# Gate rows written from SyncE's queue, eight weight tiles asked for from ScalarE's

## The chip, the core and the metric

The kernel runs on one core of a Trainium2 chip (trn2). Its time is the device time in microseconds (us) of one execution, as the median of several runs. The engines are named as the profile names them: PE is TensorE's matmul, PEld its weight load, DVE VectorE, ACT ScalarE, POOL GpSimd, SP SyncE. DMA transfers are asked for on three queues, which the profile numbers: q1 is SP's, q10 is ACT's, q0 is POOL's. An engine that asks for a transfer spends time of its own on that (its issue); the data move later, on 16 DMA engines which all queues share.

## The reference

One layer on 256 tokens of width 2048: a retention group beside a recurrent group, cross-attention over 256 memory rows, a PEER feed-forward, and a final norm. The change lies in PEER. For each token 8 heads pick 16 of 16384 single-neuron experts by product keys:

```
sub_scores = jnp.einsum('thcd,hckd->thck', q, sub_keys)
vals, ids = lax.top_k(sub_scores, PEER_TOPK)
cand = vals[:, :, 0, :, None] + vals[:, :, 1, None, :]
top_sc, pos = lax.top_k(cand.reshape(t, PEER_HEADS, ...), PEER_TOPK)
eid = (i1 * PEER_N_KEYS + i2).reshape(t, PEER_HEADS * PEER_TOPK)
gate = jax.nn.softmax(top_sc, axis=-1).reshape(t, PEER_HEADS * PEER_TOPK)
...
act = jax.nn.gelu(jnp.einsum('td,tkd->tk', xb, u_tab[eb]))
out = jnp.einsum('tk,tkd->td', gb * act, v_tab[eb])
```

## The kernel before

The tables are U and V, 16384 rows of 2048 each, taken as 128 columns of 128 experts. The kernel computes the first `RD = 40` columns for every token whether or not they were picked ("the eager pass"), then up to 32 more columns chosen by how often they were picked, and gathers the remaining picked rows one by one.

**The eager pass of U** (`u_chunk`, `u_block`, lines 1190 and 151) takes the 40 columns as 80 weight tiles of 128 x 1024 f32, 512 KB each. A tile is loaded into one of four `raw` buffers (`raw_tile`, line 128, on SP's queue); ACT casts it to a high half (line 137), DVE makes the low half (line 138), and PE multiplies both (line 158, 24 matmuls a tile). Two tiles make a column; ACT then applies gelu (line 1198). A `raw` buffer is free again when the low half of its tile is made, so a tile is asked for up to four tiles ahead of its use.

**The weave.** After each half column (one tile) `wv.pump` runs some of the waiting side work, generators that yield what they cost: the credit is `RG = 8.0` a tile while the gates are built, and 3.5 (`RK`) in the stage behind it. First in this queue is `route` with `gbuild`, then `side`.

**`gbuild`** (line 1131) builds the gates of all tokens, 64 steps of 4 tokens. A step compares indices on DVE (line 1149), scales on POOL (1150), casts on ACT (1152), multiplies on PE (1163 gates, 1166 counts) and copies the product out on ACT (1169, 1170). It costs 1.3 and 0.3 of credit. Eight steps are a group of 32 tokens (`GT`), and at its end (step `m % 8 == 7`, line 1171) the group's gates go to DRAM in three writes: `gd` (line 1173, 384 KB) and twice `rows`, a view of `gt` (lines 1175 and 1176, 384 KB and 1024 KB, in runs of 32 floats). So there are 8 groups and 24 writes, all on ACT's queue. A group then scales two finished columns on DVE (line 1181, 0.3 of credit each).

**`side`** (line 1117) follows: `choose` picks the 32 further columns; `look_up` (line 1009) finds in 8 steps, 4 for each half of the tokens, which picks these cover. Before it, POOL loads index rows of 1 MB each (`at_load`, line 1005: steps 0 to 3 early, 4 and 5 as `side` starts, 6 and 7 behind look-ups 0 and 1, into the buffers of look-ups 0 and 1). Each look-up is 32 matmuls (line 1017) and two DVE operations (1023, 1025). The normed rows `hn` are read back in two reads of 1 MB on SP's queue, into buffers that a look-up has read before: `h[0]` behind the fourth look-up (line 1021) and one of the `kept` tiles behind the sixth (line 1027). Behind each half of the look-ups DVE picks the rows still to be gathered (lines 941 and 942), and POOL gathers the first three of them, 1 MB each (line 1063, issued at line 1474). The 33rd column (tiles 65 and 66) may get its gelu only once all look-ups are done (line 1196). The products of these rows with the normed tokens (line 1481) come later and read `h[0]`.

**Order.** In this part of the kernel no order is written out by hand: the framework's planner takes the program in the order in which it was emitted and puts an instruction into its engine's queue where, by the planner's own estimate, its inputs and buffers are ready; among ready ones the earlier emitted goes first. On the chip each engine works its queue in that order, and one that waits holds all behind it. The part from line 1813 on is ordered by hand, and is not touched.

Of the kernel before, what the change touches and what calls it, by code (L numbers as in the profile page):

```python
# [18 lines left out]
P = 128  # L19
D = 2048  # L20
KB = D // P
T = 256
# [18 lines left out]
SPILL_AT = (8, 14)  # L41
LOOK_AT = (20, 30, 40, 50)
EARLY = 3
SWAP = 8
WARM = 18
RD = 40
# [6 lines left out]
GT = 32  # L53
# [36 lines left out]
def hybrid_layer_kernel(ctx: ExitStack, tc: tile.TileContext, a: dict, out: bass.AP, dbg=None):  # L90
    nc = tc.nc
    V, A, G, PE = nc.vector, nc.scalar, nc.gpsimd, nc.tensor
# [21 lines left out]
    def slot(tag, shape, name, dt=F32):  # L114
        return b8.tile(shape, dt, tag=tag, name=name, bufs=3 if tag == "ms" else 2)
# [5 lines left out]
    def sm(name):  # L121
        return ps2_.tile([P, 512], F32, tag="sm", name=name)
# [2 lines left out]
    iota = cp.tile([P, P], F32, name="iota")  # L125
    ones = cp.tile([P, P], F32, name="ones")

    def raw_tile(src):
        t = ws.tile([P, 1024], F32, tag="raw", name="raw", bufs=4)
        nc.sync.dma_start(t, src)  # L130
        return t

    def split(raw, hi=None, lo=None):
# [17 lines left out]
    def u_block(srcs, pt):  # L151
        for j, src in enumerate(srcs):
            hi, lo = split(raw_tile(src))
            for part in range(3):
                for k in range(8):
                    kb = 8 * j + k
                    x = xn[:, kb, T:] if part == 1 else xn[:, kb, :T]
                    PE.matmul(pt[:, :T], (lo if part == 2 else hi)[:, k * P:(k + 1) * P], x,  # L158
                              start=(part == 0 and kb == 0), stop=(part == 2 and kb == KB - 1))
            wv.pump(wv.rate)  # L160

    def whalf(j, src, xt, pt, raw=None):
        hi, lo = split(raw_tile(src) if raw is None else raw)
        w_mms(j, hi, lo, xt, pt)
        wv.pump(wv.rate)
# [329 lines left out]
    for i in range(3):  # L495
        t = slot("qs" if i == 0 else "ms", [P, TT, 1024], "qkv"[i])
# [321 lines left out]
    def route():  # L818
# [76 lines left out]
        for tt in range(TT):  # L895
# [31 lines left out]
            yield from finish(tt)  # L927
        wv.rate = RG
        gates = gbuild()
        tr["t"] = rp.tile([P, P + 1], F32, tag="cand", name="tri")  # L930
        nc.sync.dma_start(tr["t"], a["tri"])
# [59 lines left out]
    def at_of(i):  # L991
        return ats[i].bitcast(BF16).rearrange("p (s t) -> p s t", t=P)

    def compare(i):
        at = at_of(i)
        for n in range(0, 32, 16):
            V.tensor_scalar(at[:, n:n + 16], at[:, n:n + 16], tr["t"][:, P:], None, op0=ALU.is_equal)
            yield 0.7
# [6 lines left out]
    def at_load(i):  # L1005
        tt, c = divmod(i, 4)
        G.dma_start(ats[i].bitcast(BF16), i1d[tt, 32 * c:32 * c + 32].rearrange("s t -> (s t)")[None, :].to_broadcast([P, 32 * P]))

    def look_up(tt):
        fl = gx["b"][:, 1920:2048]  # L1010
        for c in range(4):
            at = at_of(4 * tt + c)
            if tt:
                yield from compare(4 * tt + c)
            pt = sm("look")
            for n in range(32):
                PE.matmul(pt[:, NW * n:NW * n + NW], at[:, n], words, start=True, stop=True)
            if not tt and c < 2:
                at_load(6 + c)
            if 4 * tt + c == 3:  # L1020
                nc.sync.dma_start(h[0], hn[:P, :])
            found = gx["b"][:, 512:512 + 32 * NW].rearrange("p (s w) -> p s w", w=NW)
            V.tensor_tensor(found, pt[:, :32 * NW].rearrange("p (s w) -> p s w", w=NW),
                            which[tt][:, 32 * c:32 * c + 32], op=ALU.mult)
            V.tensor_reduce(fl[:, 32 * c:32 * c + 32], found, axis=AX.X, op=ALU.add)
            if 4 * tt + c == 5:
                nc.sync.dma_start(held_in[NCH + NDY - 1], hn[P:2 * P, :])
            yield 1.0
        fu = fl.bitcast(U32)
        V.tensor_copy(fl.bitcast(I32), fl)  # L1030
        V.tensor_tensor(fu, fu, bits[tt], op=ALU.logical_shift_right)
        V.tensor_scalar(fu, fu, 31, None, op0=ALU.logical_shift_left)
        for t in (key[tt], work[tt]):
            V.tensor_tensor(t.bitcast(U32), t.bitcast(U32), fu, op=ALU.bitwise_or)
        yield 1.0
# [90 lines left out]
    gd = dp.tile([NCH - ND, P, T // GT, 8, GT], F32, name="gd")  # L1126
# [4 lines left out]
    def gbuild():  # L1131
        prev = None
        cnt["t"] = pcn.tile([P, 512], F32, tag="cnt", name="cnt")
        rows = gt_.rearrange("(r p) t -> p r t", p=P)
        for n in range(T // 4 + 1):
            if n in LOOK_AT:
                yield from compare(LOOK_AT.index(n))
            nxt = None
            tt, t0 = divmod(4 * n, P)
            ss = slice(t0, t0 + 4)  # L1140
            if n < T // 4:
                h0, q0 = n % 3 * 512, n % 3 * 256
                four = gx["b"][:, 1536:1792].bitcast(BF16).rearrange("p (a b) -> p a b", b=4)
                o1 = gx["a"][:, h0:h0 + 512].rearrange("p (a b) -> p a b", a=4)
                c1, o2 = (gx["d"][:, k + q0:k + q0 + 256].bitcast(BF16).rearrange("p (a b) -> p a b", b=4)
                          for k in (0, 768))
                og = gx["b"][:, h0:h0 + 512].rearrange("p (a b) -> p a b", a=4)
                for o, ix in ((o2, rT), (c1, i1T)):
                    V.tensor_tensor(o, four, ix[tt][:, None, ss].to_broadcast([P, P, 4]), op=ALU.is_equal)  # L1149
                G.tensor_tensor(og, o2.rearrange("p a b -> p b a"), gtT[tt][:, ss, None].to_broadcast([P, 4, P]),  # L1150
                                op=ALU.mult)
                A.copy(o1, c1.rearrange("p a b -> p b a"))
                nxt = (o1, o2, og, c1)
                yield 1.3
            if prev:
                o1, o2, og, c1 = prev
                m = n - 1
                k = m % (GT // 4)
                if k == 0:
                    ga, gb = slot("qs", [P, P // 2, GT], "gs"), gbs[m // (GT // 4) % 2]  # L1160
                pt = sm("G")
                for j in range(4):
                    PE.matmul(pt.rearrange("p (c t) -> p c t", t=4)[:, :, j], o1[:, j], og[:, j],  # L1163
                              start=True, stop=True)
                for j in range(4):
                    PE.matmul(cnt["t"][:, :RS], c1[:, :, j], o2[:, RD:, j], start=(m == 0 and j == 0),  # L1166
                              stop=(m == T // 4 - 1 and j == 3))
                ks = slice(4 * k, 4 * k + 4)
                A.copy(ga[:, :, ks], pt[:, :T].rearrange("p (c t) -> p c t", t=4))
                A.copy(gb[:, :, ks], pt[:, T:].rearrange("p (c t) -> p c t", t=4))  # L1170
                if k == GT // 4 - 1:
                    ts = slice(4 * m + 4 - GT, 4 * m + 4)
                    A.dma_start(gd[:, :, m // (GT // 4)].rearrange("q p c t -> p q c t"),
                                ga[:, 8 * ND:RD].rearrange("p (q c) t -> p q c t", c=8))
                    A.dma_start(rows[:, :P // 2 - RD, ts], ga[:, RD:])
                    A.dma_start(rows[:, P // 2 - RD:, ts], gb)
                    for i in range(ND):
                        while f"u{i}" not in done:
                            yield 3.0
                        av = acts[i][:, :, ts]  # L1180
                        V.tensor_tensor(av, ga[:, 8 * i:8 * i + 8], av, op=ALU.mult)
                        yield 0.3
                yield 0.3
            prev = nxt
        done.add("gbuild")
# [294 lines left out]
    def dot(tt, k, gat, last, k0=0, rows=None):  # L1480
        V.scalar_tensor_tensor(junk, gat, 1.0, h[0] if rows is None else rows, op0=ALU.mult, op1=ALU.mult, accum_out=coef[tt][:, k:k + 1])  # L1481
        if k % 8 == 7 or k == last:
            s = slice(max(k - k % 8, k0), k + 1)
            A.activation(coef[tt][:, s], coef[tt][:, s], AF.Gelu_apprx_tanh)
            V.tensor_tensor(coef[tt][:, s], coef[tt][:, s], sel2[tt][:, s], op=ALU.mult)
# [20 lines left out]
    def chosen():  # L1506
# [19 lines left out]
        for kind, tt, k, gs in ops:  # L1526
# [8 lines left out]
            if kind == "dot":  # L1535
                dot(tt, k, mine[0], BASE - 1, rows=held_in[NCH + NDY - 1] if tt and k < SWAP else None)
                if tt == 0 and k == BASE - 1:
# [231 lines left out]
    row_ops = chosen()  # L1769
    for _ in range(EARLY):  # L1770
        next(row_ops)
# [138 lines left out]
```

## Time and profile before

| | |
|---|---|
| median of 3 runs | 1966.1 us (1964.4 to 1967.62) |
| the profiled execution | 1966.72 us |
| its span, first to last instruction | 1964.9 us |
| mean granted TensorE clock | 0.985 |
| the three lines of gate writes, first and last issue | 1031.7 and 1158.7 us |
| bytes moved by DMA | 502.01 MB, mean 255 GB/s |
| chain that ended last, by engine | PE 62%, DMA 16%, DVE 9%, issue 7%, POOL 3% |

All times of the trace count from the span's start. A row of a timeline gives the start, the duration, the engine (with a q where it is the engine's queue that issues a DMA), the line, the operation, what it writes and reads, and in brackets the idle time before it and what ended that. "raw<-in_U_dram" is a load of a U tile, "gd<-gs" and "gt<-gs" are the gate writes, "h<-hn" and "kept<-hn" the reads of normed rows, "kept<-i1d" and "h<-i1d" the index rows, "U<-xn,hi" the products of the eager pass. In rows by stage the first number is the stage's length, then follow the busy times of PE, PEld, DVE, ACT and POOL with the instructions in parentheses, the granted clock, the DMA engines' share and GB/s.

### The profile page before, as it was taken

To read this page: it belongs to the slowest core of one execution; us is meant where nothing else is said; L and a number is where in the kernel's file an instruction comes from. 1 tells how busy PE (TensorE), PEld (TensorE's weight loads), DVE (VectorE), ACT (ScalarE), POOL (GpSimd) and SP (SyncE) were. 2 spreads that over 40 slices of the span, in tenths; PEclk is the share of its full clock that TensorE was granted. 3 is DMA by queue.
4 is the path that set the end of the run, shared out by engine and by line. 5 is a ranking of instruction groups with operands and counts; after the bars stand their busy time and mean duration, and the time that the engine had idled before them with its cause. 6 is when DMAs were issued, how large, how long until landed. Compare 5 with 4: busy or idle time off the path is not lost.

```text
span 1964.9 us, 28497 instructions
## 1 busy us (share of the span) xinstructions
PE 1888.0 (96%) x10644; PEld 1584.1 (81%) x10644; DVE 1499.5 (76%) x2304; ACT 850.5 (43%) x1324; POOL 526.3 (27%) x370
## 2 busy tenths in 40 slices
PE   9999999999999999999999877999999979999998
PEld 8888888888889988899999877988888768556563
DVE  6877968654566656899996757799889879687856
ACT  6566444544555555545455532333334433111121
POOL 0200010000000000000115431356443578587823
PEclk9999999999999999999999988999999999999999
DMA  8775665566664556755768787899898989989992
GB/s 292 269 224 170 210 197 181 150 190 192 184 191 151 152 161 202 278 171 165 240 190 156 156 250 242 301 407 361 326 392 329 356 329 409 378 329 416 421 408 93
DMA packets 203534, 502.01 MB, mean 255 GB/s; under 512 B 106792, under 2 KB 113064, under 8 KB 174888
## 3 DMA queue, kind: packets, MB, share of 16 engines
q1 hardware_dynamic: 72720, 257.38, 40.0%
q0 software_dynamic: 36096, 227.24, 29.5%
q10 hardware_dynamic: 94576, 15.54, 4.9%
q8 instruction: 84, 1.38, 0.3%
q14 instruction: 58, 0.48, 0.1%
HBM read 505.34 MB, written 21.30 MB: 268 GB/s over the span
## 4 chain that ended last, share of the span: by engine, by line
PE 62%; DMA 16%; DVE 9%; issue 7%; POOL 3%; ACTq 1%; ACT 1%; POOLq 0%; SPq 0%; DVEq 0%
PE wb L147 11%; PE xc L200 7%; PE xc L201 7%; PE xc L203 7%; PE U L158 7%; PE wb L149 6%; DMA gs<-in_Us_dram,idx 3%; DMA at<-in_Us_dram,idx 3%; PE acc L1658 3%; PE acc L1232 3%; DMA h<-in_Vs_dram,idx 2%; DVE lo L138 2%; PE G L1163 2%; DMA kept<-gt,dyn 2%; DMA raw<-in_V_dram 1%
## 5 line engine op out<-in xcount | busy, mean ns | idle before, releaser
L138 DVE TENSOR_TENSOR lo<-raw,hi 128x1024 fp32r<-128x1024 f32 x364 | 448.7, 1234 | 222.2 <-PE xc L203 122.6
L137 ACT CAST hi<-raw 128x1024 fp32r<-128x1024 f32 x364 | 381.8, 1052 | 351.0 <-PE xc L201 174.4
L158 PE MATMUL U<-xn,hi 128*128 128x256 f32 x1280 | 177.2, 290 | 15.0 <-ACT hi L137 15.0
L158 PEld LDWEIGHTS U<-xn,hi 128*128 128x128 f32 x1280 | 165.1, 197 | 15.5 <-ACT hi L137 15.5
L147 PE MATMUL U<-xn,hi 128*128 128x512 f32 x512 | 139.8, 406 | 0.0
L796 POOL DMA_DIRECT2D hn<-h x2 | 1.1, 560 | 509.0 <-DVE h L794 509.0
L1402 ACT CAST hi<-kept 128x1024 fp32r<-128x1024 f32 x52 | 53.6, 1051 | 184.1 <-DMA kept<-in_Vs_dram,dyn 90.0
L147 PE MATMUL wb<-hT,hi 128*128 128x512 f32 x448 | 116.9, 396 | 0.0
L1232 PE MATMUL acc<-kept,kept 128*128 128x512 f32 x256 | 110.2, 592 | 0.0
L1150 POOL TENSOR_TENSOR kept<-kept 128x512 f32<-128x512 bf16 x64 | 72.0, 1133 | 128.5 <-DVE kept L1149 89.4
L1489 DVE SCALAR_TENSOR_TENSOR hh<-gs,coef,hh 128x2048 f32<-128x2048 f32 x32 | 75.2, 2349 | 40.9 <-DMA gs<-in_Vs_dram,idx 40.5
L1481 DVE SCALAR_TENSOR_TENSOR junk<-gs,h 128x2048 bf16<-128x2048 f32 x43 | 98.2, 2285 | 8.8 <-DMA gs<-in_Us_dram,idx 8.8
L147 PEld LDWEIGHTS U<-xn,hi 128*128 128x128 f32 x512 | 92.6, 191 | 15.3
L158 PE MATMUL U<-xn,lo 128*128 128x256 f32 x640 | 97.1, 297 | 7.3 <-DVE lo L138 7.1
L1232 PEld LDWEIGHTS acc<-kept,kept 128*128 128x128 f32 x256 | 48.6, 190 | 60.4 <-issue 60.3
L158 PEld LDWEIGHTS U<-xn,lo 128*128 128x128 f32 x640 | 87.6, 203 | 10.3 <-DVE lo L138 10.0
L147 PEld LDWEIGHTS wb<-hT,hi 128*128 128x128 f32 x448 | 80.6, 189 | 13.9
L1149 DVE TENSOR_TENSOR kept<-kept,kept 128x512 bf16<-128x512 bf16 x128 | 63.3, 543 | 36.7 <-PE cnt L1166 27.1
L147 PE MATMUL wb<-xT,hi 128*128 128x512 f32 x352 | 89.4, 394 | 0.8 <-ACT hi L137 0.8
L1419 DVE TENSOR_TENSOR lo<-uT,hi 128x512 fp32r<-128x512 f32 x128 | 81.8, 681 | 7.3 <-ACT hi L1400 7.1
L1474 POOL DMA_INDIRECT gs<-in_Us_dram,idx x49 | 56.8, 1160 | 101.3 <-DVE junk L1481 91.1
L200 PE MATMUL xc<-hi,xT 128*128 128x512 f32 x192 | 76.3, 398 | 0.0
(512 smaller groups left out, 4505.6 us busy)
## 6 DMA issues: line engine op xcount, KB each, us to landing
raw<-in_U_dram SPq DMA_DIRECT2D x80, 512.0 KB, 5.2
raw<-in_w_qkv_dram SPq DMA_DIRECT2D x48, 512.0 KB, 3.6
raw<-in_w_xyg_dram SPq DMA_DIRECT2D x44, 512.0 KB, 4.1
raw<-in_V_dram SPq DMA_DIRECT2D x44, 512.0 KB, 6.6
raw<-in_w_xk_dram SPq DMA_DIRECT2D x32, 512.0 KB, 3.7
raw<-in_w_xv_dram SPq DMA_DIRECT2D x32, 512.0 KB, 3.7
raw<-in_w_out_dram SPq DMA_DIRECT2D x32, 512.0 KB, 3.6
raw<-in_w_xq_dram SPq DMA_DIRECT2D x32, 512.0 KB, 3.7
```

The lines of the kernel that those rows point to most:

```text
L137: A.copy(hi, raw)
L138: V.tensor_tensor(lo, raw, hi.bitcast(F32), op=ALU.subtract)
L147: PE.matmul(pt, hi[:, ks], xt[:, kb, :], start=(kb == 0), stop=(kb == KB - 1))
L149: PE.matmul(pt[:, :T], lo[:, ks], xt[:, kb, :T], start=False, stop=False)
L158: PE.matmul(pt[:, :T], (lo if part == 2 else hi)[:, k * P:(k + 1) * P], x, start=(part == 0 and kb == 0), stop=(part == 2 and kb == KB - 1))
L200: PE.matmul(pt, xh, hi[:, w], start=(n == 0 and k == 0), stop=False)
L201: PE.matmul(pt, xl, hi[:, w], start=False, stop=False)
L203: PE.matmul(pt, xh, lo[:, w], start=False, stop=(n == 7 and k == 1))
L1232: PE.matmul(acc[dc][tt], av[:, c, tt * P:(tt + 1) * P], row[:, dc * 512:(dc + 1) * 512], start=False, stop=False)
L1419: V.tensor_tensor(los[t][:, s], pts[t][n], his[t][:, s].bitcast(F32), op=ALU.subtract)
L1481: V.scalar_tensor_tensor(junk, gat, 1.0, h[0] if rows is None else rows, op0=ALU.mult, op1=ALU.mult, accum_out=coef[tt][:, k:k + 1])
L1489: V.scalar_tensor_tensor(hh[tt], gat, coef[tt][:, k:k + 1], hh[tt], op0=ALU.mult, op1=ALU.add)
```

## The change

Three edits. The three gate writes of each group are issued on SP's queue instead of ACT's. When the last group's writes have been emitted, the next eight U tiles in the order of emission are asked for on ACT's queue instead of SP's. The two reads of normed rows are emitted behind the eighth look-up instead of behind the fourth and the sixth.

```
+TURN = 8
...
+    turn = []
+
     def raw_tile(src):
         t = ws.tile([P, 1024], F32, tag="raw", name="raw", bufs=4)
-        nc.sync.dma_start(t, src)
+        (turn.pop() if turn else nc.sync).dma_start(t, src)
         return t
...
-            if 4 * tt + c == 3:
+            if 4 * tt + c == 7:
                 nc.sync.dma_start(h[0], hn[:P, :])
...
-            if 4 * tt + c == 5:
+            if 4 * tt + c == 7:
                 nc.sync.dma_start(held_in[NCH + NDY - 1], hn[P:2 * P, :])
...
-                    A.dma_start(gd[:, :, m // (GT // 4)].rearrange("q p c t -> p q c t"),
+                    nc.sync.dma_start(gd[:, :, m // (GT // 4)].rearrange("q p c t -> p q c t"),
                                 ga[:, 8 * ND:RD].rearrange("p (q c) t -> p q c t", c=8))
-                    A.dma_start(rows[:, :P // 2 - RD, ts], ga[:, RD:])
-                    A.dma_start(rows[:, P // 2 - RD:, ts], gb)
+                    nc.sync.dma_start(rows[:, :P // 2 - RD, ts], ga[:, RD:])
+                    nc.sync.dma_start(rows[:, P // 2 - RD:, ts], gb)
+                    if m == T // 4 - 1:
+                        turn.extend([A] * TURN)
```

## The prediction

> **What bounds the kernel now.** I read the page's engine lines first, then busy time by stage around the lines that the diff touches, then the timelines of ScalarE (ACT), TensorE (PE), SyncE's queue (SP) and VectorE (DVE) in the one stage where PE is not full, and last the DMA table of that stage.
>
> ```profile
> PE 1888.0 (96%) x10644; PEld 1584.1 (81%) x10644; DVE 1499.5 (76%) x2304; ACT 850.5 (43%) x1324; POOL 526.3 (27%) x370
> ```
> ```profile
> 1138.00:1157.00 19.00, 17.19 (x142) 16.94 (x141) 10.28 (x17) 11.13 (x28) 7.10 (x8) 0.91 0.81 154
> 1157.00:1182.00 25.00, 12.02 (x237) 11.55 (x235) 11.67 (x36) 0.79 (x2) 2.98 (x5) 0.70 0.95 349
> 1182.00:1251.00 69.00, 59.94 (x492) 58.96 (x492) 53.27 (x188) 19.88 (x27) 12.40 (x9) 0.89 0.75 243
> 1260.00:1340.00 80.00, 79.34 (x514) 70.96 (x513) 73.72 (x94) 29.21 (x65) 43.79 (x31) 1.00 1.00 403
> ```
>
> PE bounds the whole. By stage (length; busy PE, PEld, DVE, ACT, POOL; granted clock; DMA share; GB/s) it is nearly full in the last of the eight gate groups (17.19 of 19 us) and again behind 1260 (79.34 of 80), but it idles 13.0 us between 1157 and 1182 and 9.1 us from there to 1251. The change acts here, so in this stretch it can win 22.0 us at most. Why PE idles stands on ACT (start, duration, line, what it is, idle time before it and what ended that):
>
> ```profile
> 1158.73 22.43 ACTq L1176 DMA_DIRECT2D gt<-gs  x1
> 1181.21 0.38 ACT L1198 ACTIVATE kept<-U 128x256 f32<-128x256 f32 x1 [24.21 <-DMA gt<-gs]
> 1181.49 3.88 ACT L137 CAST hi<-raw 128x1024 fp32r<-128x1024 f32 x4
> 1187.90 0.38 ACT L1198 ACTIVATE kept<-U 128x256 f32<-128x256 f32 x1 [2.54 <-PE U L158]
> 1192.12 1.05 ACT L137 CAST hi<-raw 128x1024 fp32r<-128x1024 f32 x1 [3.83 <-DMA raw<-in_U_dram]
> 1195.41 1.04 ACT L137 CAST hi<-raw 128x1024 fp32r<-128x1024 f32 x1 [2.24 <-DMA raw<-in_U_dram]
> ```
> ```profile
> 1169.34 1.20 PE L1017 MATMUL look<-words,kept 128*128 128x11 bf16 x31
> 1182.58 3.79 PE L158 MATMUL U<-xn,hi 128*128 128x256 f32 x16 [12.05 <-ACT hi L137]
> ```
> ```profile
> 1190.58 0.56 PE L1017 MATMUL look<-words,h 128*128 128x11 bf16 x16
> 1190.99 4.08 PE L158 MATMUL U<-xn,hi 128*128 128x256 f32 x32
> 1196.51 2.18 PE L158 MATMUL U<-xn,hi 128*128 128x256 f32 x16 [1.44 <-ACT hi L137]
> ```
>
> The last gate write holds ACT for 22.43 us in its issue alone. Four loaded weight tiles lie there meanwhile: their casts run back to back at 1181.49, and PE waits 12.05 us for the first. The two casts after these wait for DMA. The other seven writes of this kind cost ACT about 3.2 us (three lines, least, median and most in ns), and the DMA table from 1160 to 1176 says why the last does not (queue, packets, MB, share of the engines' time):
>
> ```profile
> L1173 ACTq DMA_DIRECT2D gd<-gs x8: 366/367/384, 1031.7 to 1156.8; - x8
> L1175 ACTq DMA_DIRECT2D gt<-gs x8: 501/501/1474, 1032.2 to 1157.2; - x8
> L1176 ACTq DMA_DIRECT2D gt<-gs x8: 2946/3182/22435, 1032.7 to 1158.7; - x8
> ```
> ```profile
> q0 software_dynamic: 606, 4.46, 67.8%
> q1 hardware_dynamic: 338, 2.00, 30.2%
> q10 hardware_dynamic: 536, 0.07, 2.7%
> ```
>
> ACT's queue (q10) got 536 packets through in those 16 us, beside 4.46 MB of POOL's (q0) and 2.00 MB of SP's (q1), together 0.40 MB/us. The next two rows are q10's from 1050 to 1064, an undisturbed group, and from 1177 to 1190:
>
> ```profile
> q10 hardware_dynamic: 11696, 1.84, 75.7%
> ```
> ```profile
> q10 hardware_dynamic: 9761, 1.25, 62.9%
> ```
>
> So the write waits for the large transfers to end and then needs some 13 us for 9761 packets.
>
> **The change part by part.** *Which tiles move.* I number the U tiles of the eager pass 1 to 80.
>
> ```profile
> raw<-in_U_dram SPq DMA_DIRECT2D x80, 512.0 KB, 5.2
> ```
> ```profile
> 1157.18 0.33 SPq L130 DMA_DIRECT2D raw<-in_U_dram  x1
> 1165.01 0.33 SPq L1021 DMA_DIRECT2D h<-hn  x1
> 1170.56 0.33 SPq L1027 DMA_DIRECT2D kept<-hn  x1
> 1183.81 47.81 SPq L130 DMA_DIRECT2D raw<-in_U_dram  x13
> ```
>
> Through the weave's credits (8.0 for each half block, 1.6 for a gate step, 0.6 more at a group's end) the last gate write is emitted behind tile 59, so the eight requests that go to ACT are tiles 60 to 67. 80 - 13 = 67: these are just the tiles that SP had asked for before the long write, the last of them at 1157.18. Tiles 68 to 80, the thirteen from 1183.81 on, stay on SP, now behind the gate write.
>
> *Writes off ACT, groups 1 to 7.* 0.37 + 0.50 + 3.18 = 4.05 us each, 28.4 us of ACT in all. PE's one regular gap in a group is this:
>
> ```profile
> 1141.73 0.50 PE L1166 MATMUL cnt<-kept 128*128 128x88 bf16 x4 [1.81 <-DVE kept L1149]
> ```
>
> It is ended by DVE. I take 0; if ACT were behind DVE's lateness after all, 7 x 1.81 = 12.7 us would be the upper end.
>
> *Writes on SP, groups 1 to 7.* SP is held 4.05 us a group, and tile requests behind the write wait for ACT's copies into the gate buffers too. Who waits for that is the cast of a tile four places later. A group of 19 us spends 13.4 credits at 8.0 a tile, so it uses under two tiles, and a request is some 38 us ahead of its use, against 4.05 us of issue and the undisturbed write's 13 us of data. I take 0. Without that lead it would be up to 17 us a group.
>
> *Eight requests on ACT.* About 0.37 us each (the shortest ACT row above), 3 us in all, in a stage where ACT is busy 11.13 of 19 us. Each waits until DVE has made the low half of the tile four places earlier, and gate copies and casts queue behind it on ACT. DVE's low half takes 1.22 us (rows below), so 0 to 9.8 us for eight, hidden in ACT's 7.9 idle us of each group; I take 0.
>
> *The last write.* Freed, ACT casts tiles 64 to 67 at once, and PE goes on at 1170.5 instead of 1182.6. How far it gets:
>
> ```profile
> 1235.50 15.72 PE U L158 x130
> ```
>
> 0.121 us a matmul. Up to the end of the 32 at 1190.99 there were two whole tiles of 24 and 32 more, 80 matmuls or 9.7 us, and half a look-up of 0.56: PE is there at 1180.8 instead of 1195.1. What is late next is tile 69, whose cast at 1195.41 ended the 1.44 us gap before 1196.51. Its request now stands on SP behind the write and perhaps behind the two reads. As those reads (2.0 MB, 5.0 us at 0.40 MB/us) no longer run beside the key loads, the write gets through 5.0 us sooner: issue done at 1176.2 instead of 1181.2, data at about 1185 instead of 1190. Tile 70's transfer, in the chain of waits, shows what one takes in traffic:
>
> ```profile
> 1203.01 8.86 DMA raw<-in_U_dram
> 1211.95 1.05 ACT hi L137
> ```
>
> The bounds for tile 69's cast: 1185, if it needs those 8.9 us from 1176.2 on; and 1200, if it comes behind all data of the write (1185), both reads (5.0), tiles 68 and 69 (1.05 MB, 2.6) and three row reads that share the engines (below, 7 us). I take 1192, near the middle, because at least the write's rest is ahead of it on its queue: 3.4 us won, bounds +10.4 and -4.6. The Trainium skill's page DMA: Bandwidth & Descriptors (section Queues, rings and completion order) says that on each DMA engine the descriptors of one ring are consumed in order; by that rule tile 69 comes in the later half, which is the first rival below. No row here shows two such transfers in one queue.
>
> *What moves up with it.* DVE stood 8.92 us before tile 64's low half, and its picks of the first block lay behind that; the row reads that need them go out at 1195.69, and fill the engines from 1196 to 1212 (third row, q0):
>
> ```profile
> 1182.56 1.22 DVE L138 TENSOR_TENSOR lo<-raw,hi 128x1024 fp32r<-128x1024 f32 x1 [8.92 <-ACT hi L137]
> ```
> ```profile
> 1195.69 0.99 POOL L1474 DMA_INDIRECT at<-in_Us_dram,idx  x1 [10.73 <-issue]
> ```
> ```profile
> q0 software_dynamic: 576, 4.19, 69.7%
> ```
> ```profile
> 1213.02 1.22 DVE L138 TENSOR_TENSOR lo<-raw,hi 128x1024 fp32r<-128x1024 f32 x1 [4.08 <-ACT hi L137]
> ```
>
> They start some 10 us sooner, so that tile 70 no longer shares with them: 5.2 us (median of the 80) instead of 8.9, 3.7 us won, between 0 and the 4.08 that DVE waited for it.
>
> *Two reads later.* Both are emitted behind the eighth look-up, but what they wait for (look-ups 4 and 6) is unchanged, and the planner puts a request where it is ready: tile 67, emitted later than the first read, is ahead of it on SP. So their place may not change at all; the long write holds them anyway. Their first reader is far off:
>
> ```profile
> 1239.11 2.29 DVE L1481 SCALAR_TENSOR_TENSOR junk<-at,h 128x2048 bf16<-128x2048 f32 x1
> ```
>
> 1239 against a landing near 1190: 0, with 49 us of cover.
>
> *Behind 1251.* All later work starts from the picks and the end of the U pass, so what is won here is taken to carry over whole.
>
> Sum: 3.4 + 3.7 = 7.1 us. The profiled execution took 1966.7 (span 1964.9), 0.6 over the median of the runs, 1966.1; so 1966.1 - 7.1 = 1959.0 us.
>
> **The rivals.** *The stall only moves* (0.24): tile 69 is cast at 1195 as before, tile 70 still shares; 0 to 3.9 us won, 1964.5. For it: PE runs dry at 1180.8, and all that it needs next stands on SP behind the write. Against it: 2.0 MB and 4 MB leave the window.
>
> *The whole stall goes* (0.14): tiles 68 and 69 come ahead of the reads at 1185 and, because ACT casts sooner, the planner puts the low halves of 66 and 67 ahead of the picks, so tile 70 is asked for before PE needs it. 10.4 + 4.1 = 14.5 us won, 1951.6.
>
> *Slower: weights stuck behind the write* (0.17). If the write's data end at 1190 as now, because this read, which waits for tile 64's low half, comes sooner and takes the room that the two reads left,
>
> ```profile
> 1183.95 1.01 POOL L1250 DMA_INDIRECT row<-in_Us_dram,dyn  x1 [18.50 <-DVE lo L138]
> ```
>
> then reads 5.0, tiles 2.6 and shared row reads 7 give 1204.6 for tile 69, 9.2 us later than now, less 3.7: 1971.6. It decides from the point at which tile 69's cast falls behind about 1199.
>
> *ACT is held all the same* (0.02, counted with no change): if a long issue on SP also blocked requests on ACT, tile 67's would stand 20 us before the casts, and the time stays 1966. Against it: SP's requests at 1165.01 and 1170.56 took 0.33 us each in the middle of ACT's 22.43. The Trainium skill's page Perfetto Trace Analysis (section DMA Instruction, HWDGE) says that descriptor generation is one block, shared by two sequencers and locked for one instruction at a time; by that rule this rival would hold, and those two rows speak against it.
>
> **How the numbers follow.** About 0.2%, 3.9 us, is what a measurement of this kernel can tell from no change. The forecast has 0.43. Faster is forecast and whole stall, 0.57; the same is 0.24 + 0.02 = 0.26; slower 0.17. The range leaves out under half of the whole-stall case, which spreads to both sides of 1951.6, and half of the slower one, around 1971.6: 1950 to 1971.
>
> **What would show it.** Right: no ACT gap over 5 us near 1160, casts of tiles 64 to 67 before 1168, a long SP issue of the last write ending near 1176, PE's stall now before tile 69 with an end by 1193, row reads near 1185, and the end of the U products, now 1235.50 + 15.72 = 1251.2, near 1244. Wrong: tile 69 cast behind 1199, an ACT request that waits for DVE while PE idles in groups 4 to 8, or a gain by 1251 that the end of the span does not show.

## The result and the profile after

The changed kernel takes 1941.46 us (median of 4 runs, 1938.14 to 1946.75) against 1966.86 us of the kernel before (4 runs), a ratio of 0.9875 with a 95% interval of 0.9859 to 0.9891. 25 us are won; 7 were forecast.

The first rows are stages of the changed kernel (length; busy PE, PEld, DVE, ACT, POOL; granted clock; DMA share; GB/s): the gate stage, one group of it, and the stretch from there to the end of the U products. The second fence has the two stages of the kernel before.

```profile
1031.00:1138.00 107.00, 106.21 (x975) 105.70 (x974) 92.59 (x149) 81.78 (x187) 64.20 (x57) 1.00 0.91 181
1122.00:1138.00 16.00, 16.00 (x149) 15.84 (x149) 13.35 (x31) 11.33 (x28) 8.31 (x9) 1.00 0.93 180
1138.00:1226.30 88.30, 73.90 (x766) 72.65 (x764) 63.36 (x210) 21.61 (x30) 15.35 (x12) 0.90 0.86 292
```

```profile
1031.00:1157.00 126.00, 115.12 (x1012) 112.65 (x1012) 82.46 (x135) 77.31 (x188) 61.38 (x56) 0.97 0.79 154
1157.00:1251.60 94.60, 72.16 (x729) 70.51 (x727) 64.94 (x224) 21.03 (x29) 15.38 (x14) 0.84 0.80 272
```

The larger part came where the forecast had put nothing. The gate stage is 19 us shorter (107 instead of 126), the stretch behind it 6.3. Part of that is work moved from the one to the other: PE did 1012 matmuls in the longer stage and does 975 in the shorter, so 37 of them, about 4.5 us at 0.121, are done later. The two stretches together, 220.6 and 195.3 us, are a sum that no such shift touches: PE was idle for 33.3 us of the first and is for 15.2 of the second (18.1 us less), and its busy time falls from 187.3 to 180.1 us (7.2 less) for the same 1741 matmuls, because fewer of them run at a lower granted clock (0.97 and 0.84 in the two stages before, 1.00 and 0.90 with the change). 18.1 + 7.2 = 25.3 us; the last gelu of the eager pass ends at 1226.3 instead of 1251.6, and the span is 25.6 shorter (1939.3 against 1964.9). What was won by the end of the U products carried over whole. In the gate stage alone, 10.1 of the 19 us are idle time of PE (10.9 before, 0.8 with the change), some 4.5 are the 37 matmuls moved, and the rest, about 4, can be put down to the clock. Less traffic is not the reason: the DMA share of the stage is higher with the change, 0.91 against 0.79.

**How a group looked, and how it looks now.** Three views of the kernel before, in one late group: PE, then DVE, then ACT.

```profile
1129.50 3.74 PE L1163 MATMUL G<-kept,kept 128*128 128x128 f32 x32
1136.83 1.22 PE L1166 MATMUL cnt<-kept 128*128 128x88 bf16 x12
1143.66 1.91 PE L158 MATMUL U<-xn,lo 128*128 128x256 f32 x8
1147.80 1.12 PE L158 MATMUL U<-xn,lo 128*128 128x256 f32 x8
```

```profile
1133.67 0.76 DVE L1149 TENSOR_TENSOR kept<-kept,kept 128x512 bf16<-128x512 bf16 x2 [4.27 <-PE cnt L1166]
1139.75 1.59 DVE L1181 TENSOR_TENSOR kept<-gs,kept 128x256 f32<-128x256 f32 x2
1141.26 3.96 DVE L1149 TENSOR_TENSOR kept<-kept,kept 128x512 bf16<-128x512 bf16 x9
```

```profile
1139.07 3.15 ACTq L1176 DMA_DIRECT2D gt<-gs  x1
1142.27 0.67 ACT L1152 CAST kept<-kept 128x512 f32<-128x512 bf16 x1 [3.95 <-DVE kept L1149]
```

PE's queue had the G products of four steps in a row (32 matmuls); meanwhile DVE stood 4.27 us for a count that gives it back its buffer; later it had the scaling of two columns and nine compares to make one after the other, and PE stood 1.81 us for one of them (the row of 1141.73 in the prediction). ACT made no cast for the next step until 1142.27, just as its write's issue ended; but the row puts that wait down to DVE's compare, and PE's gap had ended before, at 1141.73, with the issue still running. So by these rows the gap comes from the order of the queues and not directly from ACT being held. Behind two of the five gaps of 1.81 us the next matmuls ran at the lower clock: the same eight take 1.91 us at 1143.66 and 1.12 at 1147.80. The same stretch of PE's timeline in the changed kernel:

```profile
1129.89 1.06 PE L1166 MATMUL G<-kept,kept 128*128 128x128 f32 x8
1130.79 0.49 PE L1169 MATMUL cnt<-kept 128*128 128x88 bf16 x4
1131.10 1.10 PE L1166 MATMUL G<-kept,kept 128*128 128x128 f32 x8
1132.04 0.49 PE L1169 MATMUL cnt<-kept 128*128 128x88 bf16 x4
```

One step's G, one step's counts, and no gap over 0.8 us in the whole stage. Nobody wrote this order: the planner, which no longer had some 4 us of issue to place on ACT in each group, made it. The order goes with the large writes in all traces of this case: in the four kernels that issue them from ACT in groups 1 to 7 (the one before and three of the experiments), PE's G products stand in rows of up to 24 or 32 matmuls; in all others nearly every row has 8, one step.

**Behind the gates.** SP's queue in the changed kernel, then the gaps that PE has left, then ACT's casts of tiles 68 to 70:

```profile
1066.25 7.60 SPq L133 DMA_DIRECT2D raw<-in_U_dram  x2
1138.88 8.64 SPq L1179 DMA_DIRECT2D gt<-gs  x1
1152.85 13.10 SPq L1024 DMA_DIRECT2D h<-hn  x1
1166.04 2.19 SPq L133 DMA_DIRECT2D raw<-in_U_dram  x3
1168.40 0.52 SPq L1030 DMA_DIRECT2D kept<-hn  x1
```

```profile
1146.81 1.00 PE L1020 MATMUL look<-words,h 128*128 128x11 bf16 x32 [6.13 <-DVE best L988]
1177.02 2.66 PE L161 MATMUL U<-xn,hi 128*128 128x256 f32 x16 [3.32 <-ACT hi L140]
1199.00 0.79 PE L161 MATMUL U<-xn,lo 128*128 128x256 f32 x2 [3.73 <-DVE lo L141]
```

```profile
1172.48 1.05 ACT L140 CAST hi<-raw 128x1024 fp32r<-128x1024 f32 x1 [9.61 <-DVE kept L1028]
1175.92 1.05 ACT L140 CAST hi<-raw 128x1024 fp32r<-128x1024 f32 x1 [2.39 <-remote]
1179.08 1.05 ACT L140 CAST hi<-raw 128x1024 fp32r<-128x1024 f32 x1 [2.11 <-DMA raw<-in_U_dram]
```

The 12.05 us stall is gone, and three smaller ones stand in its place. The last write's issue takes 8.64 us on SP, but the request behind it, the first read of normed rows, then takes 13.10 where such a request took 0.33 before: the write still fills the queue (4494 packets of SP's queue go through between 1153 and 1166, beside 3.99 MB of POOL's), only the row that shows it is another. Tile 68 is asked for at 1166.04, behind both.

### The profile page after: what moved, and what is told of

It is laid out like the page before. It is cut to its first block, busy times and chain, and to the rows that moved or that the text cites. A ratio compares the mean times of both kernels' runs of the same rounds, so it can differ in the third digit from the quotient of the medians.

```text
span 1939.3 us, 28503 instructions
## 1 busy us (share of the span) xinstructions
PE 1884.1 (97%) x10644; PEld 1580.8 (82%) x10644; DVE 1509.6 (78%) x2304; ACT 857.0 (44%) x1324; POOL 523.1 (27%) x370
## 4 chain that ended last, share of the span: by engine, by line
PE 63%; DMA 15%; DVE 11%; issue 7%; POOL 2%; ACT 1%; SPq 0%; POOLq 0%; DVEq 0%; ACTq 0%
PE wb L150 10%; PE xc L203 7%; PE xc L204 7%; PE xc L206 7%; PE U L161 6%; PE wb L152 5%; DMA gs<-in_Us_dram,idx 5%; PE G L1166 3%; PE acc L1663 3%; PE acc L1237 3%; DVE lo L141 3%; DMA h<-in_Vs_dram,idx 2%; DMA raw<-in_V_dram 1%; DMA kept<-gt,dyn 1%; PE acc L1218 1%
## 5 line engine op out<-in xcount | busy, mean ns | idle before, releaser
L1407 ACT CAST hi<-kept 128x1024 fp32r<-128x1024 f32 x52 | 53.9, 1053 | 180.1 <-DMA kept<-in_Vs_dram,dyn 75.5
L1153 POOL TENSOR_TENSOR kept<-kept 128x512 f32<-128x512 bf16 x64 | 74.1, 1157 | 106.5 <-DVE kept L1152 105.6
L150 PEld LDWEIGHTS wb<-hT,hi 128*128 128x128 f32 x448 | 80.6, 189 | 14.4 <-ACT hi L140 0.4
L1152 DVE TENSOR_TENSOR kept<-kept,kept 128x512 bf16<-128x512 bf16 x128 | 75.6, 640 | 7.4 <-PE cnt L1169 6.4
L1215 PE MATMUL acc<-hi,xe 128*128 128x512 f32 x192 | 76.4, 398 | 0.0
```

Of the source, the lines that this page charges most:

```text
L150: PE.matmul(pt, hi[:, ks], xt[:, kb, :], start=(kb == 0), stop=(kb == KB - 1))
```

## The experiments

The kernel before took medians of 1964.8 to 1966.9 us beside these runs. "Last count" is the start of the last count matmul (L1166, now L1169): 1156.3 before, 1134.2 with the change. PE's work on the gates ends with the last count or the last G product, whichever is later (the order differs): at 1156.6 before, at 1137.1 with the change. A trace shows one execution, which can lie some us off the median of its run: 1949.43 us with only the writes moved, 1981.11 with only the requests, 1964.01 with only the last group, 1938.75 and 1955.39 with the late reads, with and without requests on ACT.

**One part at a time.** Theory A: the writes of groups 1 to 7 are the larger part. Theory B: it is the second queue for the tiles.

Only the writes on SP: the change without

```
-                    if m == T // 4 - 1:
-                        turn.extend([A] * TURN)
```

and with the reads of normed rows at their old place.

> Of the change only the three gate writes of every group on SyncE's queue: no weight tile is asked for from ScalarE, the two reads of normed rows stand where they stood. Theory A (gate groups): what the prediction put at nothing, the writes of groups 1 to 7 off ScalarE, is the larger part; with ScalarE free of 4.05 us of issue a group the eight groups take some 15.3 us each instead of 17.9, PE's 1.81 us gaps go, the last count of the gate stage comes near 1134 us instead of 1156, and 16 us are won before anything at the last write is counted; some of the 9 us behind it may be lost, since tiles 60 to 67 now wait on SP behind the writes: 1941 to 1952 us. Theory B (second queue): the gate stage is faster because the weight tiles are asked for from another queue than the writes, so without that the SP queue blocks the tiles: gate stage as before or longer, 1960 us or more.

Measured: 1941.1 us, ratio 0.9869 (0.9847 to 0.9891), as much as the whole change. Last count at 1138.7, but the gates end at 1139.0, only 1.9 us behind those of the change.

```profile
1031.00:1138.00 107.00, 105.46 (x966) 104.92 (x965) 89.81 (x136) 81.74 (x188) 64.88 (x56) 1.00 0.88 179
```
```profile
1179.08 5.28 PE L161 MATMUL U<-xn,hi 128*128 128x256 f32 x23 [12.05 <-ACT hi L140]
```

The gate stage runs through without ACT's requests: B falls. Behind it the trace has a stall of 12.05 us, at another place than before and as long by chance. It is the trace of the slowest of the four executions (1949.43 us); whether the other three had this stall is not known.

Only the requests on ACT: the kernel before with `raw_tile` as in the change and

```
+                    if m == T // 4 - 1:
+                        turn.extend([A] * TURN)
```

> Of the change only the eight weight tiles asked for from ScalarE; all gate writes stay on ScalarE, the reads of normed rows stand where they stood. Theory A: nothing is won in the gate stage (gaps of 1.81 us stay, last count near 1156) and the last write holds ScalarE as before: 1963 to 1969 us. Theory B: the gate stage shortens, last count near 1134 to 1140, and 12 us or more are won: 1955 us or less.

Measured: 1970.7 us, 1.0026 (1.0009 to 1.0042), just above the range of A: the requests alone win nothing and lose a little. Four of the five gaps of 1.81 us stay.

Only the last group's writes on SP, with the other two edits:

```
+                    (nc.sync if m == T // 4 - 1 else A).dma_start(...
```

(so for each of the three writes)

> The change, but the writes of groups 1 to 7 stay on ScalarE; only the last group's writes are on SyncE. Theory A: the gate stage stays as before (last count near 1156, gaps of 1.81 us), and only what the last write cost is won, 9 us: 1957 us, 1953 to 1961. Theory B: the writes of groups 1 to 7 cost nothing, and the time is that of the whole change, 1941 us, or below 1948.

Measured: 1968.83 us, 1.0022 (1.0009 to 1.0034). Stage, then SP, ACT and PE:

```profile
1031.00:1157.00 126.00, 112.64 (x972) 109.27 (x971) 83.73 (x146) 74.48 (x183) 62.57 (x57) 0.96 0.71 134
```
```profile
1158.63 22.70 SPq L1179 DMA_DIRECT2D gt<-gs  x1
1181.49 7.02 SPq L1024 DMA_DIRECT2D h<-hn  x1
1188.61 1.03 SPq L133 DMA_DIRECT2D raw<-in_U_dram  x2
```
```profile
1168.56 0.33 ACTq L133 DMA_DIRECT2D raw<-in_U_dram  x1
1202.11 1.04 ACT L140 CAST hi<-raw 128x1024 fp32r<-128x1024 f32 x1 [17.11 <-DMA raw<-in_U_dram]
1205.88 1.04 ACT L140 CAST hi<-raw 128x1024 fp32r<-128x1024 f32 x1 [2.73 <-DMA raw<-in_U_dram]
```
```profile
1206.98 2.50 PE L161 MATMUL U<-xn,hi 128*128 128x256 f32 x10 [15.71 <-ACT hi L140]
```

The gate stage is as slow as before, as A says. But the 9 us that A gave to the last write are not won, and the run is even a little slower than the kernel before: this is close to the prediction's slower rival as it was written down. Tiles 68 and 69 come behind a write whose issue ends at 1181.3, tile 69 is cast at 1205.88 (the rival said 1204.6), and PE stands 15.71 us. The Trainium skill's page DMA: Bandwidth & Descriptors (section Queues, rings and completion order) has descriptors of one ring consumed in order. This run neither bears that out nor speaks against it: when tile 68 is asked for, at 1188.61, the write is nearly through (8105 packets on SP's queue from 1181 to 1189, 733 from then to 1202), and the tile is cast 13.5 us later, beside 3.53 MB of POOL's row reads. ACT's request of 0.33 us at 1168.56, in the middle of SP's 22.70, shows once more that a long issue on one queue does not lock the other.

All groups but the last on SP, the last on ACT (`A if m == T // 4 - 1 else nc.sync`), the other two edits kept:

> The change, but the last group's writes stay on ScalarE; only groups 1 to 7 write from SyncE. Theory A: the gate stage is as short as with the change (last count near 1134 to 1139), and the last write holds ScalarE as before, so that tiles 64 to 67 or their like wait for it: the 16 us of the gate stage are won, the 9 us behind it are not: 1950 us. Theory C (behind the gate stage the DMA engines are full, and it does not matter which queue the last write is on): 1939 to 1945 us.

Measured: 1946.78 us, 0.9893 (0.9874 to 0.9912), between A and C. Last count at 1133.8. ACT:

```profile
1138.15 8.55 ACTq L1179 DMA_DIRECT2D gt<-gs  x1
1154.76 23.99 ACTq L133 DMA_DIRECT2D raw<-in_U_dram  x1
```

The writes of groups 1 to 7 alone (with the two other edits, which win nothing by themselves) are worth 1966.4 - 1946.8 = 19.6 us. With them on SP, moving the last one too wins about 5 more, though the two intervals overlap. Here again the write's own issue is short, and a tile request behind it on the same queue is held, 23.99 us.

**What about ACT's issue costs.** The change, with two of the three writes repeated from ACT in groups 1 to 7:

```
+    gt2 = dp.tile([NS, T], F32, name="gt2")
...
+                    if m < T // 4 - 1:
+                        rows2 = gt2.rearrange("(r p) t -> p r t", p=P)
+                        A.dma_start(rows2[:, :P // 2 - RD, ts], ga[:, RD:])
+                        A.dma_start(rows2[:, P // 2 - RD:, ts], gb)
```

> The whole change, and in groups 1 to 7 ScalarE writes the same 88 rows a second time into a scratch tensor that nobody reads (two of the three writes; 11,264 records of 128 bytes a group): ScalarE's issue is back, some 3.7 us a group, and 1.44 MB of traffic a group are added. Theory A: the gate stage is as long as before (last count 1152 to 1158), 14 to 18 us of the gain are lost: 1955 to 1961 us. Theory B: ScalarE's issue is hidden, so only the traffic could cost: below 1947 us.

Measured: 1997.29 us, 1.0165 (1.0138 to 1.0193).

```profile
1031.00:1157.00 126.00, 101.10 (x816) 97.78 (x815) 71.20 (x117) 64.37 (x157) 55.09 (x49) 0.86 0.99 171
```

The direction is A's, the size far beyond it, and the DMA share of 0.99 says why: this run loads the DMA engines too. It does not settle what ACT's issue costs. It does show the planner's part: with two large writes on ACT again, G products stand in rows of three steps (24 matmuls) again.

The change, with three small writes from ACT instead (in the place of the two above):

```
+                        for r in range(3):
+                            A.dma_start(rows2[:, r:r + 1, ts], ga[:, r:r + 1])
```

> The whole change, and in groups 1 to 7 ScalarE also issues three small writes a group (one row of 128 partitions by 32 numbers each, 384 records of 128 bytes a group instead of 11,648) into a scratch tensor that nobody reads. PE's queue as built keeps the order of the changed kernel (G of one step, then its counts, 64 times) where the kernel before has G of four steps in a row. Theory A1 (what cost was the time that ScalarE is held, and the order that follows from it): ScalarE is held about 1.2 us a group in pieces of 0.4, no gaps come back: 1941 to 1944 us. Theory A2 (any DMA issued from ScalarE in the gate stage costs, whatever its size): the 1.81 us gaps return, 1950 us or more.

Measured: 1945.33 us, 0.9891 (0.9873 to 0.9910).

```profile
1031.00:1138.00 107.00, 106.93 (x982) 106.43 (x980) 91.38 (x144) 80.58 (x188) 64.53 (x57) 1.00 0.93 181
```

The gate stage is as short as with the change (PE busy 106.93 of 107 us), so A2 falls: it is not that ACT issues a transfer, but how large it is (these three hold ACT about 1.4 us a group, 0.48 each, instead of 4.05, and PE's order stays that of the change). The 4 us above the change, not clear of the intervals, lie behind the gates, in one stall of 14.52 us.

The change, with ordinary ACT work in the place of the issue:

```
+                    if m < T // 4 - 1:
+                        for _ in range(6):
+                            A.copy(gx["a"][:, 1536:].rearrange("p (c t) -> p c t", t=GT), ga[:, :16])
```

> The whole change, and in groups 1 to 7 ScalarE makes six copies of 128x512 numbers more (0.67 us each, 4.0 us a group, the time that the writes held it), into a part of a buffer that nobody reads; in its queue they stand between its other work, not in one piece, and PE's order keeps G and counts in turn in 59 of 64 steps. Theory A1a (ScalarE's time is short as such: 11 of 19 us busy plus 4): the gate stage gets as long as before, 1952 to 1960 us. Theory A1b (it is the piece of 4 us in one, behind which the casts for PE's next steps stand, and the order made around it): ScalarE has room for 4 us in small pieces, 1941 to 1946 us.

Measured: 1949.26 us, 0.9912 (0.9893 to 0.9931), above A1b and below A1a.

```profile
1031.00:1138.00 107.00, 105.59 (x965) 104.57 (x964) 90.12 (x146) 95.97 (x222) 62.52 (x55) 1.00 0.83 162
```

By stage it is clear: the last count comes at 1134.7, and PE loses 0.6 us. The copies overlap, so one takes 0.52 us from start to start, 3.1 us a group and not the 4.0 expected, and ACT's busy time grows by 14.2 us in all, from 81.78 to 95.97. For that much ACT has room. What is lost, 8 us, is lost behind the gates (a stall of 17.49 us). So in the gate stage what hurt was the issue in one piece, with the order that the planner made around it; this follows from ruling out the other two, for the run that gave ACT a long issue again, beside the writes on SP, added traffic with it. Which share is the order and which the hold was not separated; the one group shown above speaks for the order.

**Behind the gates: what limits there.** Theory C: the DMA engines are full, so only bytes that leave the stretch help. Theory D: the chain of look-ups and picks. The changed kernel's row for the time from the last write to the picks has a DMA share of 1.02:

```profile
1139.00:1181.00 42.00, 32.55 (x442) 31.91 (x441) 30.92 (x99) 7.82 (x11) 7.92 (x8) 0.85 1.02 333
```

The change with only the two reads emitted at their old places (`== 3` and `== 5` instead of `== 7`):

> The change with the two reads of normed rows emitted where the kernel before emitted them. Every engine's queue as built is the same as in the changed kernel, names of one buffer apart: the planner puts the reads where what they wait for is ready. All theories: the same as the change, 1939 to 1945 us; a difference of more than 4 us would mean that something other than the queues' order counts.

Measured: 1941.69 us, 0.9879 (0.9856 to 0.9903). Moving the two lines did nothing, as the prediction said of this edit. The queues being the same, the trace also shows how far one execution differs from another: the wait for the first look-up is 4.38 us here and 6.13 in that of the change.

The change with the reads held back by what they wait for, not by where they are emitted:

```
                 pick(tt, b)
+                if tt and b == 0:
+                    for n, t in enumerate((h[0], held_in[NCH + NDY - 1])):
+                        V.tensor_copy(t[:, :8], sel[1][:, :8])
+                        nc.sync.dma_start(t, hn[n * P:(n + 1) * P, :])
```

The two reads behind the eighth look-up are taken out.

> The change, but the two reads of normed rows are really later: a copy of 8 columns, made behind the first pick of the second block, stands ahead of each, so that in SyncE's queue they come behind eight weight tiles (68 to 75) instead of ahead of tile 68 and behind tile 70. Theory C (behind the gate stage the DMA engines are the bound, 1.02 of their time from 1139 to 1181): 2.0 MB leave the full stretch, about 5 us, the gap of 3.32 us before tile 69 goes and tiles 68 to 70 are there 5 us sooner: 1935 to 1939 us. Theory D (what limits there is the chain of look-ups and picks, not the transfers): 1940 to 1944 us.

Measured: 1934.55 us, 0.9832 (0.9814 to 0.9850), 7 us below the change and the fastest version found. SP, then PE's longest gap but that before the first look-up:

```profile
1138.49 8.38 SPq L1179 DMA_DIRECT2D gt<-gs  x1
1152.68 30.95 SPq L133 DMA_DIRECT2D raw<-in_U_dram  x8
1185.01 0.33 SPq L1053 DMA_DIRECT2D h<-hn  x1
```
```profile
1174.20 3.00 PE L161 MATMUL U<-xn,hi 128*128 128x256 f32 x16 [2.95 <-ACT hi L140]
```

Eight tiles now go ahead of the reads; the idle time of PE behind the gates falls from 14.4 to 8.3 us. The size is C's, and so is the way in part: counted from the last group's first write, tiles 68 to 71 are cast 3.8, 2.5, 4.1 and 6.7 us sooner than in the change. But the gap before tile 69, which was to go, stays at 2.95 us. What goes is most of the one of 3.73 us at 1199.00 (0.54 here) and 1.8 us of the wait for the first look-up, which the run just above lost too, without this edit. Whether it is the 2 MB or their place ahead of the tiles on SP's queue that counts was not separated.

The change with the table of powers, for which the first look-up waited 6.13 us, read ahead of the gate stage (the first line below stands in `route`):

```
+        nc.sync.dma_start(gx["b"][:, 1792:1792 + RS], a["pow"].to_broadcast([P, RS]))
...
-        pw = gx["b"][:, :RS]
-        nc.sync.dma_start(pw, a["pow"].to_broadcast([P, RS]))
+        pw = gx["b"][:, 1792:1792 + RS]
```

> The change, and the small table of powers of two (45 KB), which the first look-up waited 6.13 us for, is read before the gate stage into a part of the buffer that is free then. Theory C (DMA engines full from 1139 on): the look-ups come 6 us sooner and with them the key loads 3 and 4, which then run beside the last gate write; its issue on SyncE grows from 8.6 to about 18 us, as in the run with only the writes moved, tile 68 waits behind it, and the 6 us come back as a stall near 1170: 1939 to 1946 us. Theory D (chain of look-ups and picks): 5 to 6 us won, 1934 to 1937 us.

Measured: 1942.65 us, 0.9885 (0.9859 to 0.9910).

```profile
1138.15 16.86 SPq L1179 DMA_DIRECT2D gt<-gs  x1
1155.17 7.39 SPq L1024 DMA_DIRECT2D h<-hn  x1
```
```profile
1182.63 2.50 PE L161 MATMUL U<-xn,hi 128*128 128x256 f32 x10 [16.94 <-ACT hi L140]
```

As C said. The look-ups come sooner, so POOL asks for its key loads 3 and 4 (index rows of 1 MB, `h<-i1d` and `kept<-i1d`) beside the write, the write's issue doubles, and the wait that was taken away comes back as a stall of 16.94 us.

Both together:

> The change with the reads of normed rows really later (behind tile 75) and the table of powers read before the gate stage. Against the run with the late reads alone (1934.6 us), which kept a gap of 4.35 us before the first look-up and one of 2.95 us before tile 69: theory C: the first goes, the second grows by as much, 1932 to 1937 us; theory D: 4 us won, 1929 to 1932 us.

Measured: 1935.04 us, 0.9844 (0.9814 to 0.9874): no more than the late reads alone, in the range of C. The gap before the first look-up is gone, and one of 12.05 us stands at 1167.7.

The late reads without the requests on ACT:

> Gate writes on SyncE and the reads of normed rows really later, but no weight tile asked for from ScalarE: tiles 60 to 67 stand on SyncE between the gate writes. If asking from ScalarE is worth nothing with the reads out of the way either, 1932 to 1938 us; if the tiles then wait behind the last write, which tile 68 and its like do in either case, up to 10 us more than with the late reads and ScalarE's requests: 1938 to 1945 us.

Measured: 1951.04 us, 0.9922 (0.9900 to 0.9944), worse than either expectation. Without the late reads the requests on ACT were worth nothing (1941.1 without, 1941.5 with), with them they are worth 16 us. The gates end at 1139.2, 2.1 us later, and three gaps stand behind them, 9.01, 3.42 and 3.76 us, the middle one put down to DVE's part of the look-ups. The first begins with tile 66: without requests on ACT it stands behind the write on SP and is cast at 1174.19 instead of 1153.32. But in the trace with only the writes moved it is as late (1177.99). Why the two edits depend on each other so much was not settled.

## Why the prediction was wrong

**The step that failed** is "Writes off ACT, groups 1 to 7": "I take 0; if ACT were behind DVE's lateness after all, 7 x 1.81 = 12.7 us would be the upper end." ACT's issue was behind DVE's lateness, by way of the queues' order: with the last group's writes left on ACT, moving the others was worth 19.6 us. The working stopped at the first releaser. DVE ended PE's gap, but DVE had itself stood 4.27 us for PE a little earlier, in an order of PE's queue that the planner had made with the writes on ACT. The upper end was wrong as well. It counted seven gaps of 1.81 us where the stage has five; with two gaps under 1 us all idle time of PE there is 10.9 us. And it counted idle time alone, though matmuls at the lower clock count as busy: the quoted row of the stage that looked full (17.19 of 19 us) has a clock of 0.91. With the same mistake the prediction drew its ceiling, "it can win 22.0 us at most", around the stretch behind 1157 alone. The Trainium skill's page DMA: Bandwidth & Descriptors (section Issuing engines are not separate DMA queues) says that issuing from several engines saves only sequencer time, which is usually small beside the transfer. What moved here was just that, 4.05 us a group, and the measurement decides: it was worth most of the change.

**Writes on SP, groups 1 to 7: 0.** Right in its result, though SP's requests behind a write take 4 to 7 us (two of them 7.60 us in the row at 1066.25); PE has no gap for a tile in the gate stage, so the lead of four tiles covers that.

**Eight requests on ACT: 0.** Right in the change, where the same gate stage comes without them. With the late reads they are worth 16 us.

**The last write and what moves up, 7.1 us.** The end of the U products was forecast at 1244 instead of 1251.2. Counted from the gate stage's end, which came 18.9 us sooner (last group's first write at 1137.87 instead of 1156.75), the U products end where they would have at 1225.9 + 18.9 = 1244.8. So the size was right, but that is luck, for the way to it was not as written. The write's issue did not end near 1176 (in these counts at 1147.5 + 18.9 = 1166.4), the read behind it was the long one, tile 69 was cast at 1194.8 instead of 1192, and tile 70, at 1198.0 instead of 1211.95, brought the most. And in the world that the prediction described, the gate stage as before and only the last write moved, this term failed too: that run came out at 1.0022 of the kernel before, a small loss, where 7.1 us were to be won.

**Which of the rivals came.** The slower one is real: moving only the last write gave its stall and its sign, if not its size (1968.83 us, and 1971.6 was said). In the change it is softened by something that the prediction had not seen: the powers table, asked for at 1136.45 on SP's queue, lands 8.22 us later, the look-ups wait 6.13 us, POOL asks for its key loads 3 and 4 only at 1148.11, and the write's issue has ended by then, though its data have not. Five of the runs (times counted from the last group's first write; "clear" is when SP has issued the request behind the write):

| | third key load asked for | long issue of the write | clear |
|---|---|---|---|
| the change | 10.2 | 8.64 | 28.1 |
| late reads | 8.8 | 8.38 | 27.4 |
| last group only | 7.5 | 22.70 | 30.9 |
| writes only | 6.3 | 18.76 | 26.8 |
| powers early | 2.7 | 16.86 | 25.4 |

All traces with the last write on SP go by this: with the third key load at 8.8 us or later the write's issue takes 8.4 to 8.6 us, with it at 7.5 or sooner 16.9 to 22.7. So the third key load goes with the row in which the time stands, and hardly with how long the queue is full: in none of these traces did "clear" leave the span of 25.4 to 30.9 us.

**Two reads later: 0.** Right, and for the reason given: the planner left them where what they wait for is ready. But "0, with 49 us of cover" missed what lay in it: really later, they are worth 7 us.

**Behind 1251: carried over whole.** Right here: 25.3 us by the end of the U products, 25.6 by the end of the span. It is no rule: in the trace of the late reads 33.5 us are won by the end of the U products and 27.9 by the end of the span.

**What would show it.** Casts of tiles 64 to 67 before 1168: right (the last at 1158.65). No ACT gap over 5 us: wrong as written, ACT idles 13.35 and 9.61 us, but for PE and DVE, not in an issue. PE's stall before tile 69: right, 3.32 us. Row reads near 1185: they go out at 1171.57, which counted as above is 1190.5. Of the signs of being wrong none came: tile 69 is cast before 1199, PE has no gap over 0.8 us in the gate groups, and the gain by the end of the U products shows in the span.

## What to carry to other kernels

Do not stop at the engine that ended a gap. Ask what that engine stood for before, and whether the order of the queues was planned around an operation that you are about to move. A stage that looks full at a granted clock of 0.91 still has time in it: add up idle time and busy time at the lower clock before drawing a ceiling. To move a transfer under a planner, change what it waits for; moving its line may change nothing. And where the DMA engines are full (1.02 here), taking one wait away moved the stall; taking a transfer out of the stretch shortened it.

## What the runs showed of the hardware

The three writes of a group (11,648 records, 11,264 of them of 128 bytes) cost their queue more than their own issue: requests that took 0.33 us elsewhere took 4 to 7 us behind them in the gate stage, 13.10 behind the last group's, and 23.99 when those were on ACT. The long time can stand in the write's row (22.70 us) or in the row of the request behind it (8.64 and 13.10), and the two must be read together. Behind a gap of 1.81 us PE's matmuls ran at the lower clock in two of five cases (eight in 1.91 us instead of 1.12).
